# A four-layer streaming encoder on one core: the schedule form of each layer's head, zero-padded values for the sliding-window heads, and the norms' running sums on VectorE

## The chip, the core and the metric

The kernel runs on one core of a Trainium2 chip. The metric is device time in microseconds (us) of one execution; lower is better. Five engines work side by side, each on its own stream of instructions: PE (matrix multiplies, with its weight loads shown as PEld), DVE (VectorE), ACT (ScalarE), POOL (GpSimd) and SP (SyncE, which issues the transfers).

## The reference

One inference step with four layers over 320 tokens (256 of a prompt, 64 of a decoding stream), model width 1024. Each layer adds three things to the residual stream x:

```python
for i in range(DEPTH):                     # DEPTH = 4
    x = x + mixer_i(rms_norm(x, g_mix[i])) # i mod 3: 0 MLA, 1 stick-breaking (SBA), 2 sliding window (SWA)
    x = x + conv_ffn(rms_norm(x, g_ffn[i]), ...)
    x = x + sigmoid(rms_norm(x, g_ple[i]) @ w_gate[i]) * (p[i] @ w_proj[i])
y = rms_norm(x, g_final)
# rms_norm(x, g) = x * rsqrt(mean(x * x) + eps) * g
```

So the mixers in order are MLA, SBA, SWA, MLA. The last product of a layer, the gated one, is called PLE below. SWA has 16 query heads on 4 key heads of width 64, with 128 cached keys for the decoding stream. All is float32.

## The kernel before

**Layout.** x is kept transposed, as eight tiles x0 to x7 of 128 features by 320 tokens (NT). Each float32 matrix product is three matmuls on operands that were split into a high and a low part (`mm3`, L202 to L204: hi by hi, lo by hi, hi by lo), 24 matmuls for a full product of 1024 features into 128. Splits of anything are one ACT instruction for the high part (L160) and one subtraction for the low part (L161).

**Weights** come in 512 KB chunks (`fetch`, L168 to L176): a transfer into wraw, ACT makes whi, and DVE or POOL makes wlo (L176). POOL gets every second or third chunk while a mixer runs (`wpool`, set from WPOOL when the mixer begins) and none at other times.

**Norms.** The scale 1/rms isn't applied to the operand: products run on x times g and their results are multiplied by R, the scale spread over 128 partitions. For the norm of the next stage `norm_piece(m)` runs as soon as x[m] is final: ACT makes h{m}hi (L305), DVE h{m}lo (L306), ACT the square sq (L314), and the running sum acc is added on POOL for m = 1 to 6 (L320; m = 0 is a copy) and on DVE for m = 7. Then `norm_sums` lets PE add acc over partitions (`col_sums`, L272) and DVE find 1/rms on three columns ncol (`newton_rsqrt`, L252 to L258, eleven short instructions); `spread` puts it on the diagonal of two tiles (DVE, L282 and L283, also named sq), lets PE multiply them by ones (L287) and ACT copy R (L290).

**PLE** (`ple`, L406) goes over m: a 24-matmul product, times R (DVE L429), tanh (ACT L430), times the embedding's product (DVE L431), added to x[m] (DVE L433), then `norm_piece(m)` for the next mixer.

**Between layers.** `prep` of the next mixer (its caches' loads, splits and transposes) is called ahead of `ple`, so in program order ahead of that norm's sums. `swa_prep` loads and splits the cached keys and values; `mla_prep` transposes cached latents (`latent_turn`, L489). Their transposes use the two PSUM tiles of tag "tp", which `col_sums` and `spread` use too.

**Order.** A scheduler orders each engine's instructions by its own estimate; at a mixer's head PE has program order instead (`manual_schedule`): one full product on h0 to h7, `norm_sums`, more products, `norm_spread`. In SWA, `values(kt, i0)` multiplies the transposed softmax tiles by the values once for each of two heads u: each round fills two "tp" tiles and ends in three splits of 64 partitions into O.

## Time and profile before

| what | value |
|---|---|
| time, median of 3 runs | 1865.1 us (1860.9 to 1867.74) |
| profiled execution: its time, its span | 1871.49 us, 1869.7 us |
| busy in the span | PE 96%, DVE 72%, ACT 52%, POOL 30% |
| PE clock, mean over the span | 0.983 of full |

PE is busy nearly all the time, so the time is PE's work at the clock it was granted, plus its gaps. The stages by time: MLA 30 to 220 us, FFN to 476, PLE to 515; SBA to 680, FFN to 913, PLE to 953; SWA to 1090, FFN to 1325, PLE to 1364; MLA to 1590, FFN to 1822, PLE to 1856, final norm to 1869.7.

### The profile page before, as it was taken

Reading aid. Unit: us, or ns where it says so; the run is one execution under the profiler, and the core shown is the slowest. Engines: PE = TensorE matmul, PEld = TensorE weight load, DVE = VectorE, ACT = ScalarE, POOL = GpSimd, SP = SyncE. Lnnn points to the kernel's source line nnn. Section 1 sums busy time; section 2 is a strip of 40 time slices with the busy share of each in tenths; the row PEclk is TensorE's granted clock in tenths of the full one; section 3 lists DMA queues with packets and bytes.
Section 4 is the critical chain, followed back from the end, with each engine's and each line's share of the span. In section 5 each row is a group of like instructions: output and inputs, shape, how many; then the busy total and the mean of one; then the engine's idle time right before and its main releaser. Section 6 shows DMA issues by size and latency. Waiting matters only on the chain.

```text
span 1869.7 us, 32633 instructions
## 1 busy us (share of the span) xinstructions
PE 1798.8 (96%) x12352; PEld 1775.2 (95%) x12352; DVE 1347.4 (72%) x2637; ACT 974.6 (52%) x1849; POOL 565.6 (30%) x834
## 2 busy tenths in 40 slices
...
GB/s 207 107 112 124 126 138 162 151 150 149 168 128 140 121 133 152 151 148 150 126 157 76 46 143 158 148 154 150 144 124 100 122 129 122 157 147 153 153 147 63
DMA packets 78126, 254.15 MB, mean 136 GB/s; under 512 B 9488, under 2 KB 18192, under 8 KB 77968
## 3 DMA queue, kind: packets, MB, share of 16 engines
...
q14 instruction: 61, 0.50, 0.1%
...
## 4 chain that ended last, share of the span: by engine, by line
PE 41%; DVE 6%; ACT 2%; issue 1%; POOL 1%; DMA 0%; DVEq 0%; SPq 0%; ACTq 0%; POOLq 0%
PE ps L202 13%; PE ps L203 13%; PE ps L204 13%; ACT whi L174 1%; DVE rsh L596 1%; DVE wlo L176 1%; PE ps L272 0%; PE ps L1188 0%; DVE PTl L161 0%; POOL wlo L176 0%; DVE h6lo L306 0%; DVE m L1165 0%; DMA ckt<-ckvT 0%; DVE m L671 0%; ACT Pr L675 0%
## 5 line engine op out<-in xcount | busy, mean ns | idle before, releaser
L174 ACT ACTIVATE whi<-wraw 128x1024 fp32r<-128x1024 f32 x450 | 474.5, 1056 | 443.0 <-PE ps L203 230.4
L176 DVE TENSOR_TENSOR wlo<-wraw,whi 128x1024 fp32r<-128x1024 f32 x381 | 471.1, 1237 | 226.5 <-ACT whi L174 219.5
L176 POOL TENSOR_TENSOR wlo<-wraw,whi 128x1024 fp32r<-128x1024 f32 x69 | 166.9, 2418 | 311.0 <-ACT whi L174 292.8
L384 POOL TENSOR_TENSOR ge<-cv,R 128x256 f32<-128x256 f32 (+1 forms) x176 | 132.8, 774 | 92.8 <-ACT cv L381 92.3
L320 POOL TENSOR_TENSOR acc<-acc,sq 128x320 f32<-128x320 f32 x72 | 77.4, 1075 | 261.6 <-ACT sq L314 259.0
L347 DVE TENSOR_TENSOR x<-x,ps 128x320 f32<-128x320 f32 x128 | 61.1, 482 | 55.7 <-PE ps L204 55.4
L379 DVE SCALAR_TENSOR_TENSOR cv<-G,cols,cv 128x322 f32<-128x322 f32 x176 | 95.9, 552 | 2.4
L388 DVE TENSOR_TENSOR af<-ge,ps 128x320 f32<-128x320 f32 x88 | 42.7, 486 | 67.6 <-POOL ge L384 67.4
L202 PE MATMUL ps<-h0hi,whi 128*128 128x320 f32 x256 | 81.1, 317 | 6.5 <-ACT h0hi L305 6.2
L203 PE MATMUL ps<-h6lo,whi 128*128 128x320 f32 x256 | 79.4, 310 | 3.3 <-DVE h6lo L306 3.3
L202 PE MATMUL ps<-h7hi,whi 128*128 128x320 f32 x256 | 79.2, 311 | 3.3 <-ACT h7hi L305 3.3
L203 PE MATMUL ps<-h0lo,whi 128*128 128x320 f32 x256 | 79.9, 312 | 0.8 <-DVE h0lo L306 0.8
L202 PE MATMUL ps<-h4hi,whi 128*128 128x320 f32 x256 | 79.6, 313 | 1.1 <-ACT h4hi L160 1.1
L203 PE MATMUL ps<-h5lo,whi 128*128 128x320 f32 x256 | 79.4, 310 | 1.2 <-DVE h5lo L161 1.2
L203 PE MATMUL ps<-h7lo,whi 128*128 128x320 f32 x256 | 79.9, 312 | 0.5 <-DVE h7lo L306 0.5
L202 PE MATMUL ps<-h1hi,whi 128*128 128x320 f32 x256 | 79.9, 312 | 0.0
L203 PE MATMUL ps<-h4lo,whi 128*128 128x320 f32 x256 | 79.7, 311 | 0.2 <-DVE h4lo L306 0.2
L203 PE MATMUL ps<-h3lo,whi 128*128 128x320 f32 x256 | 79.9, 312 | 0.0
L203 PE MATMUL ps<-h2lo,whi 128*128 128x320 f32 x256 | 79.9, 312 | 0.0
L203 PE MATMUL ps<-h1lo,whi 128*128 128x320 f32 x256 | 79.8, 312 | 0.0
L204 PE MATMUL ps<-h1hi,wlo 128*128 128x320 f32 x256 | 79.8, 312 | 0.0
L204 PE MATMUL ps<-h0hi,wlo 128*128 128x320 f32 x256 | 79.8, 312 | 0.0
...
## 6 DMA issues: line engine op xcount, KB each, us to landing
...
```

What stands on the lines that cost most here:

```text
L174: nc.scalar.activation(out=hi, in_=raw, func=AF.Copy)
L176: e.tensor_tensor(out=lo, in0=raw, in1=hi.bitcast(F32), op=ALU.subtract)
L202: mm(out, w[0], x[0], start=first, stop=False, **kw)
L203: mm(out, w[0], x[1], start=False, stop=False, **kw)
L204: mm(out, w[1], x[0], start=False, stop=last, **kw)
L320: e.tensor_tensor(out=self.nacc[:, 0:NT], in0=self.nacc[:, 0:NT], in1=sq, op=ALU.add)
L347: self.nc.vector.tensor_tensor(out=self.x[m], in0=self.x[m], in1=p[:, 0:NT], op=ALU.add)
L379: nc.vector.scalar_tensor_tensor(out=cv, in0=gt[:, k:k + GW - 2], scalar=w[k], in1=cv, op0=ALU.mult, op1=ALU.add)
L384: nc.gpsimd.tensor_tensor(out=ge[:, c], in0=cv[:, c.start + o:c.stop + o], in1=R[:, c], op=ALU.mult)
L388: nc.vector.tensor_tensor(out=af, in0=ge, in1=pu[:, 0:NT], op=ALU.mult)
L596: nc.vector.tensor_tensor(out=lo[r, :].bitcast(F32R), in0=qf[r, :], in1=hi, op=ALU.subtract)
```

## The change

- **Running sums.** All additions of acc are on DVE. For m = 7 the square is made before the operand.
- **Diagonal.** The two diagonal tiles are made in `norm_sums`, right behind the Newton steps.
- **Heads.** SBA uses a new order (`head`): its first product A on h0 to h6, the second product B on h0 and h1, the sums, B on h2 to h6, and only then h7 for both. From PLE's last m up to this head all four engines keep program order. MLA keeps its order. SWA's hand-written order is gone: the scheduler orders it.
- **Weights.** `wpool` is set behind a mixer's head (`headed`), not when the mixer begins.
- **Preparation.** `prep` is called inside `ple`, behind that norm's spread. `swa_prep` does nothing any more: SWA loads its caches itself and splits a key head's old and new columns in one go (448 columns).
- **Values.** Each of a pair of SWA heads has its own value tile, zero in the other head's 64 columns, so both heads' products add up in one PSUM tile of 128 partitions: `values` has one round with three splits of 128 partitions, and the same number of matmuls.
- **Final norm.** POOL makes -x*g, DVE multiplies six of the eight outputs by the spread's PSUM result itself, and POOL two by R.

```diff
     def spread(self, r, pool, tag, bufs=2):
+        return self.spread_mm(self.diag(r), pool, tag, bufs)
+    def diag(self, r):
...
+        return dg
...
+    def spread_mm(self, dg, pool, tag, bufs=2, sign=-1.0):
+        nc = self.nc
         p = self.ps("tp")
         for k in range(2):
             i = nc.tensor.matmul(p[:, 0:NT], self.negones, dg[k], start=k == 0, stop=k == 1)
         self.pins.append(i)
         rb = self.tile(pool, [P, NT], tag, bufs=bufs)
-        nc.scalar.activation(out=rb, in_=p[:, 0:NT], func=AF.Copy, scale=-1.0)
+        self.negR = p[:, 0:NT]
+        nc.scalar.activation(out=rb, in_=p[:, 0:NT], func=AF.Copy, scale=sign)
...
+        if m == NK - 1:
+            self.norm_square(m)
+            self.norm_operand(m)
+        else:
+            self.norm_operand(m)
+            self.norm_square(m)
+    def norm_operand(self, m):
...
+            nc.gpsimd.tensor_scalar(out=hi, in0=x, scalar1=self.col(self.ng, m), scalar2=-1.0,
+                                    op0=ALU.mult, op1=ALU.mult)
...
+    def norm_square(self, m):
+        nc = self.nc
         sq = self.tile(self.nrm, [P, NT], "sq", bufs=2)
-        nc.scalar.activation(out=sq, in_=x, func=AF.Square)
+        nc.scalar.activation(out=sq, in_=self.x[m], func=AF.Square)
         if m == 0:
             self.nacc = self.tile(self.nrm, [P, NT + DEC], "acc", bufs=1)
             nc.gpsimd.tensor_copy(out=self.nacc[:, 0:NT], in_=sq)
         else:
-            e = nc.vector if m == NK - 1 or self.wpos == 0 else nc.gpsimd
+            e = nc.vector
             e.tensor_tensor(out=self.nacc[:, 0:NT], in0=self.nacc[:, 0:NT], in1=sq, op=ALU.add)
...
+        first = [(p, [self.take(name, np.arange(k * P, k * P + P), cols) for k in range(NK)]) for p, name, cols in (A,)]
+        mm = lambda n, k: self.mm3(first[n][0], first[n][1][k], h[k], k == 0, k == NK - 1)
+        for k in range(NK - 1):
+            mm(0, k)
+        p, name, cols = B
+        first.append((p, [self.take(name, np.arange(k * P, k * P + P), cols) for k in range(NK)]))
+        for k in range(NK - 1):
+            mm(1, k)
+            if k == 1:
+                self.norm_sums(keep_sum)
+        mm(0, NK - 1)
+        mm(1, NK - 1)
+        self.norm_spread()
+        self.proj(*C, h)
...
-            self.nr = self.newton_rsqrt(v)
+            self.nr = self.diag(self.newton_rsqrt(v))
     def norm_spread(self):
         with self.tc.high_priority(AHEAD):
-            self.R = self.spread(self.nr, self.nrm, "R")
+            self.R = self.spread_mm(self.nr, self.nrm, "R")
...
-        after()
+        prep = after()
...
+            if m == NK - 1 and nxt == 1:
+                self.region.enter_context(self.tc.manual_schedule(engines=ALL))
             pp = pps[m]
             pg = self.ps("mm")
             self.proj(pg[:, 0:NT], f"pg{i}", cols, h)
+            if m == NK - 1 and nxt == 1:
+                self.more_weights()
...
+        ps = [weighed(0, n) for n in range(3)]
+        self.head(*ps)
+        self.headed(1)
         with self.tc.manual_schedule(engines=PE):
-            pq, pk = project(0, 0), project(0, 1)
-            self.norm_sums()
-            pv = project(0, 2)
+            with self.tc.high_priority(AHEAD):
+                scaled(0, 0, ps[0][0])
+                scaled(0, 1, ps[1][0])
...
-            self.norm_spread()
+            scaled(0, 2, ps[2][0])
...
     def swa_prep(self, j, pool):
...
-        for kt in range(2):
-            kf, vf = T([P, W], f"kf{kt}"), T([P, W], f"vf{kt}")
-            nc.sync.dma_start(out=kf[:, NT:W], in_=t["wkT"][kt])
-            nc.sync.dma_start(out=vf[:, NT:W], in_=t["wvT"][kt])
-            KF.append(kf)
-            VF.append(vf)
-        self.load_rot(pool)
-        for kt in range(2):
-            kh = [pair([P, W], f"K{kt}{u}") for u in range(2)]
-            for u in range(2):
-                for x in kh[u]:
-                    nc.gpsimd.memset(x[64 * (1 - u):64 * (2 - u), :].bitcast(F32), 0.0)
-                s = slice(64 * u, 64 * u + 64)
-                self.split(kh[u][0][s, NT:], kh[u][1][s, NT:], KF[kt][s, NT:])
-            K.append(kh)
-            vh = pair([P, 4, P], f"V{kt}")
-            tp = self.ps("tp")
-            nc.tensor.transpose(tp[:, 0:P], VF[kt][:, NT:W], self.ident)
-            self.split(vh[0][:, 3], vh[1][:, 3], tp[:, 0:P])
-            V.append(vh)
-        return KF, VF, K, V
+        return None
...
-        early = {}
-        def product(m, tag="mm"):
-            p = self.ps(tag)
-            return p
-        with self.tc.manual_schedule(engines=PE):
-            for n, m in enumerate((8, 10, 0, 1, 2, 3)):
-                early[m] = product(m, "mm" if n < 3 else "sc")
-                if n == 1:
-                    self.norm_sums()
-                if n == 3:
-                    self.norm_spread()
+        self.headed(2)
+        h = self.norm_finish()
+        R = self.R
+        tags = ["sc"] * 3 + ["mm"] * 3
...
         def keys(kt):
-            kf, kh = KF[kt], K[kt]
+            kf = T([P, W], "kvf", bufs=2)
+            nc.sync.dma_start(out=kf[:, NT:W], in_=t["wkT"][kt])
             rope_bias(8 + kt, project(8 + kt), kf[:, 0:NT])
             nc.sync.dma_start(out=t["o_wk"][kt], in_=kf)
+            kh = [pair([P, W], f"K{kt}{u}") for u in range(2)]
             for u in range(2):
+                for x in kh[u]:
+                    nc.gpsimd.memset(x[64 * (1 - u):64 * (2 - u), :].bitcast(F32), 0.0)
                 s = slice(64 * u, 64 * u + 64)
-                self.split(kh[u][0][s, 0:NT], kh[u][1][s, 0:NT], kf[s, 0:NT])
+                self.split(kh[u][0][s, :], kh[u][1][s, :], kf[s, :])
+            K.append(kh)
         def vals(kt):
-            vf, vh = VF[kt], V[kt]
+            vf = T([P, W], "kvf", bufs=2)
+            nc.sync.dma_start(out=vf[:, NT:W], in_=t["wvT"][kt])
             f = project(10 + kt)
             nc.scalar.activation(out=vf[:, 0:NT], in_=f, func=AF.Identity, bias=self.col(f"bq{j}", 10 + kt))
             nc.sync.dma_start(out=t["o_wv"][kt], in_=vf)
-            pv = transposes([vf[:, c:c + P] for c in (0, P, S0 - 64)])[:, 0:3 * P]
-            self.split(vh[0][:, 0:3], vh[1][:, 0:3], pv.rearrange("p (a b) -> p a b", a=3))
+            vh = [pair([P, 4, P], f"V{kt}{u}") for u in range(2)]
+            for u in range(2):
+                for x in vh[u]:
+                    nc.gpsimd.memset(x[:, :, 64 * (1 - u):64 * (2 - u)].bitcast(F32), 0.0)
+            pv = four(transposes([vf[:, c:c + P] for c in (0, P, S0 - 64, NT)]))
+            for u in range(2):
+                c = slice(64 * u, 64 * u + 64)
+                self.split(vh[u][0][:, :, c], vh[u][1][:, :, c], pv[:, :, c])
+            V.append(vh)
...
-            vv = lambda b: [x[:, b] for x in V[kt]]
+            vv = lambda u, b: [x[:, b] for x in V[kt][u]]
             i2 = slice(i0, i0 + 2)
+            p, p2 = self.ps("tp"), self.ps("tp")
             for u in range(2):
-                s = slice(64 * u, 64 * u + 64)
-                p, p2 = self.ps("tp"), self.ps("tp")
-                self.mm3(p[:, 0:256], vv(0), [flat(x[:, 4 + u]) for x in PT], True, True)
+                self.mm3(p[:, 0:256], vv(u, 0), [flat(x[:, 4 + u]) for x in PT], u == 0, u == 1)
+            for u in range(2):
                 for b in range(2):
-                    self.mm3(p[:, 256:512], vv(b), [flat(x[:, 2 * u + b]) for x in PT], b == 0, b == 1)
+                    self.mm3(p[:, 256:512], vv(u, b), [flat(x[:, 2 * u + b]) for x in PT], u + b == 0, u + b == 2)
+            for u in range(2):
                 for b in range(2):
-                    self.mm3(p2[:, 0:P], vv(2 + b), [x[:, 2 * u + b] for x in PTs], b == 0, b == 1)
-                for c, src in ((slice(0, P), p[:, 0:256]), (slice(P, SEQ), p[:, 256:512]),
-                               (slice(S0, NT), p2[:, 0:P])):
-                    self.split(o[0][s, i2, c], o[1][s, i2, c], two(src)[s])
+                    self.mm3(p2[:, 0:P], vv(u, 2 + b), [x[:, 2 * u + b] for x in PTs], u + b == 0, u + b == 2)
+            for c, src in ((slice(0, P), p[:, 0:256]), (slice(P, SEQ), p[:, 256:512]), (slice(S0, NT), p2[:, 0:P])):
+                self.split(o[0][:, i2, c], o[1][:, i2, c], two(src))
...
+    def headed(self, kind):
+        self.region.close()
+        self.wpool = WPOOL[kind]
...
-            self.wpool = WPOOL[kind]
             (self.mla, self.sba, self.swa)[kind](j, pool, prep[1])
...
-            if last:
-                self.ple(i, ple, e, lambda: self.norm_start("g_final", None, None))
-            else:
-                prep = self.prep(self.layers[n + 1])
-                self.ple(i, ple, e, lambda: self.norm_start(f"g_mix{self.layers[n + 1]}"))
+            def after():
+                if last:
+                    return self.norm_start("g_final", None, None)
+                self.norm_start(f"g_mix{self.layers[n + 1]}")
+                return self.prep(self.layers[n + 1])
+            prep = self.ple(i, ple, e, after, None if last else MIXERS[self.layers[n + 1]][0])
             self.shut(cp)
...
-        self.norm_finish()
+        self.norm_sums()
+        R = self.spread_mm(self.nr, self.nrm, "R", sign=1.0)
         for m in range(NK):
             y = self.tile(self.hp, [P, NT], f"h{m}hi", bufs=1)
-            if m % 3 == 2:
-                nc.gpsimd.tensor_tensor(out=y, in0=self.fin[m], in1=self.R, op=ALU.mult)
+            if m % 4 == 2:
+                nc.gpsimd.tensor_tensor(out=y, in0=self.fin[m], in1=R, op=ALU.mult)
             else:
-                nc.vector.tensor_tensor(out=y, in0=self.fin[m], in1=self.R, op=ALU.mult)
+                nc.vector.tensor_tensor(out=y, in0=self.fin[m], in1=self.negR, op=ALU.mult)
```

How the order of instructions moves, at three places. In the rows the number at a name's end only tells buffers apart; line numbers of the changed kernel differ (L179 is L176, L205 to L207 are L202 to L204, L275 is L272, L325 is L306, L344 is L320, L486, L488 and L490 are L429, L431 and L433).

DVE at the end of the first layer's PLE, before: from h5's low part to the last sum.

```order
L306 SCALAR_TENSOR_TENSOR h5lo_6264<-x_13_97,gains_73,h5hi_6263 128x320
L431 SCALAR_TENSOR_TENSOR G_1278_6301<-G_1278_6301,ps_6170 128x320
L433 TENSOR_TENSOR x_14_99<-x_14_99,G_1278_6301 128x320
L429 TENSOR_TENSOR G_1286_6344<-ps_6313,R_5941 128x320
L306 SCALAR_TENSOR_TENSOR h6lo_6307<-x_14_99,gains_73,h6hi_6306 128x320
L431 SCALAR_TENSOR_TENSOR G_1286_6344<-G_1286_6344,ps_6220 128x320
L433 TENSOR_TENSOR x_15_101<-x_15_101,G_1286_6344 128x320
L306 SCALAR_TENSOR_TENSOR h7lo_6350<-x_15_101,gains_73,h7hi_6349 128x320
L320 TENSOR_TENSOR acc_6012<-acc_6012,sq_6353 128x320
```

The same place now, from the weight chunk ahead of h5's low part on (that chunk's wlo was POOL's before).

```order
L179 TENSOR_TENSOR wlo_6349<-wraw_6346,whi_6348 128x1024
L325 SCALAR_TENSOR_TENSOR h5lo_6264<-x_13_97,gains_73,h5hi_6263 128x320
L344 TENSOR_TENSOR acc_6012<-acc_6012,sq_6267 128x320
L488 SCALAR_TENSOR_TENSOR G_1278_6301<-G_1278_6301,ps_6170 128x320
L486 TENSOR_TENSOR G_1289_6352<-ps_6315,R_5906 128x320
L490 TENSOR_TENSOR x_14_99<-x_14_99,G_1278_6301 128x320
L488 SCALAR_TENSOR_TENSOR G_1289_6352<-G_1289_6352,ps_6220 128x320
L325 SCALAR_TENSOR_TENSOR h6lo_6307<-x_14_99,gains_73,h6hi_6306 128x320
L490 TENSOR_TENSOR x_15_101<-x_15_101,G_1289_6352 128x320
L344 TENSOR_TENSOR acc_6012<-acc_6012,sq_6310 128x320
L344 TENSOR_TENSOR acc_6012<-acc_6012,sq_6357 128x320
L325 SCALAR_TENSOR_TENSOR h7lo_6361<-x_15_101,gains_73,h7hi_6360 128x320
```

Three sums came to DVE here, the second half of m = 7's chain stands directly around h6's low part, and h7's low part is last.

PE at the head of SBA, before: the end of the first product, the sums, and the second product's begin.

```order
L202 MATMUL ps_6393<-h6hi_6306,whi_6316 128x320
L203 MATMUL ps_6393<-h6lo_6307,whi_6316 128x320
L204 MATMUL ps_6393<-h6hi_6306,wlo_6317 128x320
L202 MATMUL ps_6393<-h7hi_6349,whi_6316 128x320
L203 MATMUL ps_6393<-h7lo_6350,whi_6316 128x320
L204 MATMUL ps_6393<-h7hi_6349,wlo_6317 128x320
L272 MATMUL ps_6424<-ones_112,acc_6012 128x2 x3
L202 MATMUL ps_6450<-h0hi_6006,whi_6365 128x320
```

Now: the same first product stops at h6, and h7 comes 15 matmuls after the sums' three (at the "..." stand the rest of the second product's rows on h0 to h6).

```order
L207 MATMUL ps_6368<-h6hi_6306,wlo_6274 128x320
L205 MATMUL ps_6369<-h0hi_6006,whi_6318 128x320
...
L207 MATMUL ps_6369<-h1hi_6057,wlo_6319 128x320
L275 MATMUL ps_6404<-ones_112,acc_6012 128x2 x3
L205 MATMUL ps_6369<-h2hi_6113,whi_6318 128x320
...
L207 MATMUL ps_6369<-h6hi_6306,wlo_6319 128x320
L205 MATMUL ps_6368<-h7hi_6360,whi_6273 128x320
L206 MATMUL ps_6368<-h7lo_6361,whi_6273 128x320
```

The first row that needs h7 moved from 2 to 24 rows behind the one that needs h6's low part, the sums' row from 5 to 8 behind it.

PE at the head of SWA. Before, one product is finished alone, as in SBA (its rows for h6 and h7, the sums, and the next product).

```order
L203 MATMUL ps_11659<-h6lo_11573,whi_11582 128x320
L204 MATMUL ps_11659<-h6hi_11572,wlo_11583 128x320
L202 MATMUL ps_11659<-h7hi_11615,whi_11582 128x320
L203 MATMUL ps_11659<-h7lo_11616,whi_11582 128x320
L204 MATMUL ps_11659<-h7hi_11615,wlo_11583 128x320
L272 MATMUL ps_11690<-ones_112,acc_11278 128x2 x3
```

Now three products are interleaved: h6's low part is first used by the 40th matmul of the stage and h7 by the 50th.

```order
L205 MATMUL ps_11736<-h0hi_11229,whi_11629 128x320
L206 MATMUL ps_11626<-h6lo_11530,whi_11496 128x320
L207 MATMUL ps_11626<-h6hi_11529,wlo_11497 128x320
L206 MATMUL ps_11681<-h6lo_11530,whi_11539 128x320
L207 MATMUL ps_11681<-h6hi_11529,wlo_11540 128x320
L206 MATMUL ps_11736<-h0lo_11230,whi_11629 128x320
...
L205 MATMUL ps_11626<-h7hi_11575,whi_11496 128x320
L275 MATMUL ps_11585<-ones_112,acc_11235 128x2 x3
L206 MATMUL ps_11626<-h7lo_11576,whi_11496 128x320
```

The first use of h6's low part moved from the 20th matmul of the stage to the 40th, and that of h7 from the 22nd to the 50th.

## Rows read from the trace of the kernel before

**Rows 1.** The page: busy shares; one costly group with PE's idle time before it.

```profile
PE 1798.8 (96%) x12352; PEld 1775.2 (95%) x12352; DVE 1347.4 (72%) x2637; ACT 974.6 (52%) x1849; POOL 565.6 (30%) x834
...
L203 PE MATMUL ps<-h6lo,whi 128*128 128x320 f32 x256 | 79.4, 310 | 3.3 <-DVE h6lo L306 3.3
```

**Rows 2.** Windows by stage: length, busy times, granted clock, DMA share, GB/s.

```profile
220.00:476.00 256.00, 254.92 (x1739) 254.53 (x1738) 173.23 (x283) 110.83 (x161) 75.46 (x155) 1.00 0.45 151
476.00:515.00 39.00, 35.46 (x236) 34.22 (x235) 32.81 (x61) 21.43 (x38) 9.42 (x10) 0.99 0.48 156
...
913.00:953.00 40.00, 36.80 (x228) 36.28 (x228) 31.53 (x60) 19.48 (x34) 8.83 (x8) 0.91 0.40 128
...
975.00:1048.00 73.00, 62.59 (x378) 59.97 (x377) 56.19 (x182) 45.88 (x145) 31.82 (x34) 0.81 0.18 59
...
1325.00:1364.00 39.00, 36.40 (x234) 35.65 (x235) 32.12 (x61) 20.11 (x35) 8.75 (x8) 0.96 0.40 135
```

**Rows 3.** Timeline 508.0 to 516.6: start, duration, engine, instruction, idle before it.

```profile
508.33 0.31 PE L204 MATMUL ps<-ph7hi,wlo 128*128 128x320 f32 x1
...
509.72 2.39 POOL L176 TENSOR_TENSOR wlo<-wraw,whi 128x1024 fp32r<-128x1024 f32 x1 [1.61 <-ACT whi L174]
...
510.12 2.33 DVE L306 SCALAR_TENSOR_TENSOR h6lo<-x,gains,h6hi 128x320 fp32r<-128x320 f32 x1 [0.33 <-ACT h6hi L305]
...
512.51 0.41 PE L203 MATMUL ps<-h6lo,whi 128*128 128x320 f32 x1 [1.09 <-DVE h6lo L306]
...
514.18 0.41 PE L202 MATMUL ps<-h7hi,whi 128*128 128x320 f32 x1 [1.11 <-ACT h7hi L305]
```

**Rows 4.** Durations by line over the whole span: min/median/max in ns.

```profile
L306 DVE SCALAR_TENSOR_TENSOR h6lo<-x,gains,h6hi x8: 535/1198/2334, 12.2 to 1586.4; 128x320 fp32r<-128x320 f32 x8
...
L431 DVE SCALAR_TENSOR_TENSOR G<-G,ps x32: 473/482/489, 484.7 to 1853.9; 128x320 f32<-128x320 f32 x32
```

**Rows 5.** Durations of the running sum's additions, the same view for tile acc.

```profile
L320 POOL TENSOR_TENSOR acc<-acc,sq x72: 861/1034/1782, 230.8 to 1852.6; 128x320 f32<-128x320 f32 x72
L320 DVE TENSOR_TENSOR acc<-acc,sq x19: 474/481/493, 8.5 to 1855.6; 128x320 f32<-128x320 f32 x19
```

**Rows 6.** PE's timeline at the column sums of the second and third PLE.

```profile
914.00 1.44 PE L272 MATMUL ps<-ones,acc 128*128 128x2 f32 x6 [2.25 <-DVE V0l L161]
...
1325.23 0.83 PE L272 MATMUL ps<-ones,acc 128*128 128x2 f32 x6 [1.23 <-DVE Vl L161]
```

**Rows 7.** Windows over two stretches at the lower granted clock.

```profile
914.00:920.80 6.80, 6.80 (x27) 6.80 (x28) 3.29 (x18) 0.00 (x0) 0.00 (x0) 0.51 0.24 77
...
514.50:517.90 3.40, 3.23 (x13) 3.13 (x13) 1.84 (x3) 1.06 (x1) 0.00 (x0) 0.50 0.08 33
```

**Rows 8.** What PE waited for, 975 to 1048: total us, times, longest.

```profile
PE ps L202 <- ACT Pr L1173: 3.4, 3, 1.9
PE ps L1188 <- DVE su L1175: 2.3, 1, 2.3
...
PE ps L202 <- DVE O0l L161: 1.2, 2, 1.0
```

**Rows 9.** Groups by line, 975 to 1048: shapes, count, busy us, mean ns.

```profile
L161 DVE TENSOR_TENSOR O0l<-ps,O0h 64x256 fp32r<-64x256 f32 x8 | 3.3, 414 | 2.0 <-ACT O0h L160 1.8
```

**Rows 10.** Timeline 1861.9 to 1863.2: the first final outputs.

```profile
1861.97 0.44 ACT L290 ACTIVATE R<-ps 128x320 f32<-128x320 f32 x1 [6.45 <-PE ps L287]
1862.44 0.49 DVE L1341 TENSOR_TENSOR h0hi<-h0lo,R 128x320 f32<-128x320 f32 x1 [1.20 <-ACT R L290]
...
1862.85 1.15 DVE L1341 TENSOR_TENSOR h1hi<-h1lo,R 128x320 f32<-128x320 f32 x1
```

**Rows 11.** What PE waited for, 476 to 490.

```profile
PE ps L287 <- DVE sq L282: 0.9, 1, 0.9
```

**Rows 12.** The page: the groups that make wlo, count, busy us, mean ns.

```profile
L176 DVE TENSOR_TENSOR wlo<-wraw,whi 128x1024 fp32r<-128x1024 f32 x381 | 471.1, 1237 | 226.5 <-ACT whi L174 219.5
L176 POOL TENSOR_TENSOR wlo<-wraw,whi 128x1024 fp32r<-128x1024 f32 x69 | 166.9, 2418 | 311.0 <-ACT whi L174 292.8
```

45 lines of the change are left out of this document (25 added, 20 removed).

## The prediction

> **What bounds the kernel now.** I read the page first: PE is busy 96% of the span, DVE 72% [rows 1]. So the time is PE's work plus what PE loses, and the change leaves PE's matmuls as they are. The most to be won is PE's idle time, 1869.7 - 1798.8 = 71 us, and what the lower clock costs, (1 - 0.983) x 1869.7 = 32 us.
>
> The windows by stage come next, to see where that loss lies. An FFN loses 1 us of 256 at full clock, and there a matmul takes 254.92 / 1739 = 0.147 us of PE [rows 2]. The loss sits around the changes of layer and in SWA: 40 - 36.8 = 3.2 us idle and (1 - 0.91) x 40 = 3.6 us of clock around the change to SWA; 10.4 idle and 0.19 x 73 = 13.9 of clock in SWA's core; 2.6 and 1.6 around the change to the last MLA; 3.5 idle around the change to SBA [rows 2].
>
> The timeline at 510 us shows why PE stops when a mixer begins. POOL's wlo runs 509.72 to 512.11; DVE's h6 low part, issued beside it, takes 2.33 us and ends when wlo ends; PE, which goes through h0 to h7 in one product, waits 1.09 us for it. x7 is then late, so h7's high part is late, and PE waits 1.11 us more [rows 3]. Alone the same DVE instruction takes 0.535 us [rows 4]. The same pair stands at the two later changes of layer: the page gives 3.3 us of waiting for h6's low part in all [rows 1], three times 1.1. PE's clock then fell to 0.50 for 3.4 us after the first of the three places [rows 7]; after the other two it did not.
>
> What POOL delays is a DVE instruction whose tensors all lie in SBUF. Those that read one tensor from PSUM never grew, 473 to 489 ns in 32 cases, POOL busy or not [rows 4]. The Trainium skill, page SBUF — State Buffer, section Who interferes with whom, says the same as a rule: a DVE instruction with two SBUF inputs and a GpSimd instruction that reads SBUF block one another, and the first keeps the way for its whole length. The trace agrees.
>
> The third kind of loss is in the PLE. The column sums wait for a "tp" tile that the next mixer's preparation holds: 2.25 us before SWA, 1.23 us before the last MLA [rows 6]. After the first PE ran 6.8 us at 0.51 of its clock, which costs half of it, 3.4 us [rows 7]; after the second the 1.6 us above.
>
> **The change, part by part.**
>
> *Sums on DVE.* 72 additions leave POOL (1.034 us each) and come to DVE at 0.481 us [rows 5]: 72 x 0.481 = 35 us more on DVE. What hides them is PE: no sum is awaited before the column sums, and DVE is idle 28% of the span. The tightest place is a PLE, DVE 32.81 of 39 us [rows 2]: six additions there are 2.9 us, within the 6.2 us left. Without cover they would cost 2.9 us per PLE. What the additions on POOL had made longer on DVE comes back to it; I don't count that. I take 0.
>
> *Change to SBA.* The POOL wlo ahead of the head goes to DVE, 1.24 us [rows 12], but it stands ahead of h5's low part and not beside h6's. PE reached its wait at 512.51 - 1.09 = 511.42. The last gate product ends at 508.6 [rows 3]; from there DVE's new order has its step times R, x6, the step with the embedding, and h6's low part, 0.4 to 0.55 us each, with tanh and h6's high part on ACT between them, some 0.5 us each: about 511.2, so the first wait goes by a margin of 0.2 us. h7 is wanted 15 matmuls after the sums (2.2 us) and is long there. Gain: 1.1 + 1.1 of waits and 1.7 of clock (half of 3.4 [rows 7]) = 3.9 us. Bounds: all of it, or only 1.1 where DVE is one wlo later. The wait of the spread in the same PLE, 0.9 us [rows 11], stays, since a wlo and splits of the caches still stand ahead of the Newton steps. The new head puts transposes of the first values close behind the products that they need; that wait the trace doesn't show, 0 to one POOL wlo (2.4 us [rows 12]); I take 0.9 as in [rows 11], the nearest wait of PE for DVE.
>
> *Change to SWA.* With no preparation the 2.25 us and the 3.4 us of clock go. The wlo on POOL stays and h6's low part will again take 2.33 us, but it is wanted 20 matmuls later (20 x 0.147 = 2.9 us) and h7 28 later (4.1 us): both waits of 1.1 us are covered. Gain 2.25 + 3.4 + 2.2 = 7.9 us; at least 5.7, if the interleaving doesn't cover.
>
> *SWA's core.* 24 low splits of 64 partitions become 12 of 128; at 0.414 us, less for the narrow third of them, DVE loses some 4.5 us of work, and ACT about as much for the high parts [rows 9]. DVE is busy 56.2 of 73 us there [rows 2] and PE waits for it and for ACT behind it: 3.4 for the exponentials, 2.3 for a softmax sum, 1.2 for the splits of the first of two rounds [rows 8], which now don't exist. Against it: the cached columns are split here now (128 more columns, four times, some 0.15 us each), two splits of values per key head in place of one, 16 fills with zeros on POOL. Bounds: two thirds of the 24 us lost there (-16), or the low clock for another 16 us (+8). I take what DVE saves, with the half of a gap that it causes at the low clock: -5.
>
> *Change to the last MLA.* The column sums no longer stand behind the preparation: 1.2 + 1.6 = 2.8 us (bounds 1.2 and 2.8). The two waits at the mixer's begin stay: its product order is as before, and the wlo that POOL no longer makes there stands on DVE between the steps of x6.
>
> *Final norm.* DVE no longer waits for ACT's R (0.44 us) and reads PSUM, so the outputs that took 1.15 us beside POOL take 0.49 [rows 10]: 0.44 + 2 x 0.66 = 1.8, less what PE and the last transfer take of it: -1.5 (bounds -0.5 and -1.8).
>
> *Sum:* -3.9 + 0.9 - 7.9 - 5 - 2.8 - 1.5 = -20.2 us. Against the profiled execution, 1871.5 - 20.2 = 1851.3; that execution lies 6.4 us above the median of the runs, so I expect **1845 us**.
>
> **The rivals.**
>
> *B: SWA gives nothing, and SBA's first wait stays.* For it: the margin of 0.2 us there, and that SWA's waits are for a chain of softmax steps which the change doesn't shorten [rows 8]. 1845 + 5 + 2.8, and up to 4 more: 1853 to 1860.
>
> *C: SWA's clock stays up.* If the waits in its core become short, most of the 13.9 us comes back: -16 in place of -5, 1834. For it: PE falls to the low clock only behind waits; against it: only 1.2 us of them certainly go [rows 8].
>
> *D: DVE's sums become the bound at the mixers' ends (slower).* The added instructions have all tensors in SBUF, and POOL still makes wlo there. If all 24 of them in the four mixers ran beside one, they would take 2.33 in place of 0.48 us, 44 us in all. DVE's 28% idle over eight output steps of 24 to 48 matmuls (28 to 56 us a mixer) is 8 to 16 us a mixer; with half of the 44 us at the wrong place and the clock low for 6.8 us behind each, the loss is 22 + 4 x 3.4 = 35 us: 1880. It decides from about four of six additions blocked in a mixer. Against it: POOL's wlo takes 167 us [rows 12] of 718 us of mixers, not quite a quarter, so some six of 24 meet one. By the skill's rule above the same follows: every such addition is open to blocking; here it would be worth some 6 us of DVE under cover.
>
> *E: nothing.* PE's stalls move to the next late thing (the gain in a PLE is waited off at the mixer's begin): 1861 to 1867. Against it: the FFNs behind run at full clock with no loss [rows 2], so time won before them isn't given back in them.
>
> **How the numbers follow.** Mine 0.55 (its own range 1837 to 1853, from the bounds of SWA, -12 to +2, which are the widest); B 0.18; C 0.12; D 0.07; E 0.08. Half a per cent, about what can be told from no change, is 9.3 us: 1855.8 and 1874.4. Faster: mine, C and half of B, 0.76. Same: the other half of B and E, 0.17. Slower: D, 0.07. The range 1831 to 1862 holds mine, B, most of C and a little of E, about 0.82.
>
> **What would show it.** In the profile after: no wait for h6's low part or h7's high part at the begin of SBA and SWA, but both still at the last MLA; column sums of the second and third PLE without a wait and their stretches at full clock; POOL with only m = 0's copy of acc; DVE's busy time some 20 to 25 us higher; in SWA's core, a granted clock above 0.81 and half as many splits into O. I am wrong if SWA's core is as long as before, if new waits for DVE stand at SBA's begin, or if additions of acc take over 1 us in most cases.

## The result and the profile after

The changed kernel takes 1849.88 us (median of 4 runs, 1847.58 to 1851.6) where the kernel before took 1863.0 beside it: ratio 0.9913, 95% interval 0.9893 to 0.9933. The two medians alone give 0.9930, which lies inside that interval. It is faster by 0.7 to 0.9%, between the 1845 that was predicted and the upper end of the range. In the 49 runs of the kernel before that were made beside the later kernels the median is 1866.9 us, so the gain is 13 to 17 us, by which of the two one takes. The two profiled executions differ by more, 1869.7 - 1848.5 = 21.2 us of span, since that of before, 1871.5 us, was longer than any of these 49. Left out of all comparisons are two runs, one of E10 (its only profiled one, so that E10 has no stages below) and one of the kernel before, which ran at a mean granted clock of 0.653 and took some 2480 us.

The page of the changed kernel, busy shares as in [rows 1]:

```profile
PE 1786.0 (97%) x12352; PEld 1762.6 (95%) x12352; DVE 1353.3 (73%) x2697; ACT 969.5 (52%) x1833; POOL 483.1 (26%) x766
```

POOL's busy time fell by 82 us, DVE's rose by 6, not by the 35 of the additions alone.

Windows of the changed kernel over the stages of [rows 2] (length, PE, PEld, DVE, ACT, POOL busy, granted clock, DMA share, GB/s):

```profile
475.00:511.00 36.00, 35.56 (x240) 34.74 (x239) 30.94 (x66) 19.89 (x36) 0.70 (x3) 1.00 0.46 151
511.00:675.00 164.00, 160.06 (x1084) 153.64 (x1083) 137.85 (x259) 123.20 (x270) 39.07 (x28) 1.00 0.37 123
...
908.00:946.00 38.00, 38.00 (x263) 38.00 (x262) 31.43 (x65) 19.90 (x34) 3.83 (x4) 1.00 0.46 153
946.00:1069.00 123.00, 112.40 (x794) 110.73 (x794) 101.25 (x275) 78.47 (x211) 50.04 (x64) 0.94 0.28 93
...
1302.00:1341.00 39.00, 37.56 (x253) 36.42 (x251) 33.24 (x70) 22.11 (x39) 0.65 (x1) 1.00 0.46 150
```

The second PLE has no loss left (38.00 of 38.00 us at full clock, where [rows 2] had 3.2 idle and 0.91). New is the second line: in SBA, where PE had hardly a gap behind the head before, it now has 3.9 us of them.

PE's timeline of the changed kernel at SBA's head (h6's low part, the column sums), and at the column sums of the second and third PLE ([rows 3, 6]):

```profile
509.76 0.41 PE L206 MATMUL ps<-h6lo,whi 128*128 128x320 f32 x1
...
511.34 0.80 PE L275 MATMUL ps<-ones,acc 128*128 128x2 f32 x6
...
910.99 0.73 PE L275 MATMUL ps<-ones,acc 128*128 128x2 f32 x6
...
1304.49 0.72 PE L275 MATMUL ps<-ones,acc 128*128 128x2 f32 x6
```

None of these rows has a wait of note in front of it (none shows an idle time in brackets): the waits of 1.09, 2.25 and 1.23 us are gone. DVE's timeline there shows why the first is:

```profile
509.15 0.55 DVE L325 SCALAR_TENSOR_TENSOR h6lo<-x,gains,h6hi 128x320 fp32r<-128x320 f32 x1
509.62 0.48 DVE L490 TENSOR_TENSOR x<-x,G 128x320 f32<-128x320 f32 x1
```

h6's low part takes 0.55 us, no longer 2.33, and PE reads it as it ends.

Durations by line in the changed kernel, answering to [rows 4, 5]: h6's low part (eight norms) and the additions of acc.

```profile
L325 DVE SCALAR_TENSOR_TENSOR h6lo<-x,gains,h6hi x8: 534/544/1993, 12.2 to 1566.9; 128x320 fp32r<-128x320 f32 x8
...
L344 DVE TENSOR_TENSOR acc<-acc,sq x91: 474/484/2699, 8.5 to 1835.9; 128x320 f32<-128x320 f32 x91
```

The median of h6's low part fell from 1198 to 544 ns. Of the 91 additions three ran beside a wlo of POOL and took 2.7 us.

What PE waited for in SWA, 941 to 1069 us of the changed kernel ([rows 8]):

```profile
PE ps L1227 <- DVE PTl L164: 6.8, 2, 5.7
PE ps L205 <- ACT Pr L1212: 2.4, 1, 2.4
PE ps L207 <- POOL Ql L164: 0.9, 1, 0.9
```

The waits for O0's splits are gone. Those for transposed softmax tiles, of which before had these,

```profile
PE ps L202 <- DVE PTl L161: 1.7, 1, 1.7
...
PE ps L1188 <- DVE PTl L161: 0.7, 2, 0.4
```

have grown into one of 5.7 us. The final outputs ([rows 10]), timeline of the changed kernel:

```profile
1841.59 0.44 ACT L301 ACTIVATE R<-ps 128x320 f32<-128x320 f32 x1 [5.76 <-PE ps L297]
...
1842.06 0.49 DVE L1386 TENSOR_TENSOR h0hi<-h0lo,ps 128x320 f32<-128x320 f32 x1 [1.19 <-ACT R L301]
1842.46 0.48 DVE L1386 TENSOR_TENSOR h1hi<-h1lo,ps 128x320 f32<-128x320 f32 x1
```

No output is stretched to 1.15 us any more, but DVE still starts only when ACT's copy ends, though it reads PSUM.

**Stages.** The comparisons below go by PE's own records: the start of the last matmul of each FFN's output (on a*hi), of each gate product (on ph7hi) and of each attention output (on O*h). In the changed kernel these starts are 469.54, 506.67, 672.13, 905.12, 941.28, 1065.64, 1298.63 and 1336.14 us. Differences of them are the lengths of stages; "end" runs from the last gate matmul to the end of the span. The stages that are left out (the two MLA stages with their FFNs, the FFNs behind SBA and SWA, the last PLE) make up the rest. In us, one profiled execution each:

| kernel | PLE0 and SBA | PLE1 | SWA | PLE2 | end | median of runs | ratio to before |
|---|---|---|---|---|---|---|---|
| before | 201.2 | 42.0 | 136.8 | 39.6 | 17.1 | 1866.9 | 1 |
| changed | 202.6 | 36.2 | 124.4 | 37.5 | 15.7 | 1849.9 | 0.9913 |
| E1 SBA's old head | 201.1 | 36.2 | 124.6 | 37.5 | 15.7 | 1848.3 | 0.9915 |
| E2 sums on POOL | 202.0 | 36.2 | 122.7 | 38.0 | 16.4 | 1850.9 | 0.9925 |
| E3 values unpadded | 202.8 | 36.2 | 130.0 | 37.4 | 16.3 | 1856.2 | 0.9953 |
| E4 preparation in front | 202.0 | 36.2 | 124.0 | 39.8 | 16.3 | 1852.5 | 0.9932 |
| E5 SWA ordered by hand | 202.8 | 36.2 | 124.8 | 37.4 | 16.3 | 1852.0 | 0.9928 |
| E6 SWA's caches in PLE | 203.2 | 36.5 | 123.6 | 37.3 | 15.7 | 1849.3 | 0.9915 |
| E7 old head, late POOL share | 200.9 | 36.2 | 123.9 | 37.4 | 16.3 | 1848.0 | 0.9904 |
| E8 sums twice | 203.0 | 36.2 | 124.4 | 37.7 | 16.1 | 1865.1 | 0.9996 |
| E9 split head | 199.6 | 36.2 | 124.1 | 37.6 | 15.7 | 1846.3 | 0.9888 |
| E11 before, preparation behind | 201.0 | 36.4 | 131.0 | 37.3 | 17.1 | 1858.8 | 0.9954 |
| E12 before, two parts | 199.6 | 36.7 | 125.2 | 37.6 | 17.1 | 1853.3 | 0.9945 |

The ratios' intervals reach 0.0013 to 0.0025 to either side, and the ratios were measured beside runs of the kernel before, so they are the safer comparison between kernels. Where an edit doesn't touch it, PLE1 repeats much better: it is 36.16 us in nine of them. SWA does not, since PE's clock falls there for 6.8 to 27.3 us, which differs from execution to execution.

### The profile page after: what moved, and what is told of

Same layout as the page of the kernel before. It is cut to its first block, busy times and chain, and to the rows that moved or that the text cites. A ratio compares the mean times of both kernels' runs of the same rounds, so it can differ in the third digit from the quotient of the medians.

```text
span 1848.5 us, 32578 instructions
## 1 busy us (share of the span) xinstructions
PE 1786.0 (97%) x12352; PEld 1762.6 (95%) x12352; DVE 1353.3 (73%) x2697; ACT 969.5 (52%) x1833; POOL 483.1 (26%) x766
## 4 chain that ended last, share of the span: by engine, by line
PE 81%; DVE 10%; ACT 5%; issue 2%; DMA 1%; POOL 1%; DVEq 0%; SPq 0%; ACTq 0%; POOLq 0%
PE ps L205 26%; PE ps L206 26%; PE ps L207 26%; ACT whi L177 2%; DVE wlo L179 1%; DVE rsh L654 1%; DMA wraw<-w 1%; PE ps L753 1%; PE ps L275 0%; ACT Pr L733 0%; PE ps L700 0%; DVE qnl L164 0%; PE ps L701 0%; DVE KR L541 0%; DVE PTl L164 0%
## 5 line engine op out<-in xcount | busy, mean ns | idle before, releaser
L179 DVE TENSOR_TENSOR wlo<-wraw,whi 128x1024 fp32r<-128x1024 f32 x385 | 475.0, 1235 | 220.3 <-ACT whi L177 213.0
L179 POOL TENSOR_TENSOR wlo<-wraw,whi 128x1024 fp32r<-128x1024 f32 x65 | 157.5, 2423 | 380.5 <-ACT whi L177 340.0
L436 POOL TENSOR_TENSOR ge<-cv,R 128x256 f32<-128x256 f32 (+1 forms) x176 | 141.4, 823 | 86.4 <-ACT cv L433 86.1
L431 DVE SCALAR_TENSOR_TENSOR cv<-G,cols,cv 128x322 f32<-128x322 f32 x176 | 97.2, 560 | 2.3
L205 PE MATMUL ps<-h0hi,whi 128*128 128x320 f32 x256 | 81.1, 317 | 6.8 <-ACT h0hi L324 6.2
L205 PE MATMUL ps<-h4hi,whi 128*128 128x320 f32 x256 | 79.8, 313 | 1.1 <-ACT h4hi L163 1.1
L205 PE MATMUL ps<-h6hi,whi 128*128 128x320 f32 x256 | 79.3, 311 | 1.0 <-ACT h6hi L324 1.0
L205 PE MATMUL ps<-h2hi,whi 128*128 128x320 f32 x256 | 79.7, 311 | 0.0
L207 PE MATMUL ps<-h1hi,wlo 128*128 128x320 f32 x256 | 79.7, 311 | 0.0
L205 PE MATMUL ps<-h1hi,whi 128*128 128x320 f32 x256 | 79.6, 311 | 0.0
L207 PE MATMUL ps<-h0hi,wlo 128*128 128x320 f32 x256 | 79.6, 311 | 0.0
```

What stands on the lines that cost most here:

```text
L179: e.tensor_tensor(out=lo, in0=raw, in1=hi.bitcast(F32), op=ALU.subtract)
L205: mm(out, w[0], x[0], start=first, stop=False, **kw)
L207: mm(out, w[1], x[0], start=False, stop=last, **kw)
L431: nc.vector.scalar_tensor_tensor(out=cv, in0=gt[:, k:k + GW - 2], scalar=w[k], in1=cv, op0=ALU.mult, op1=ALU.add)
L436: nc.gpsimd.tensor_tensor(out=ge[:, c], in0=cv[:, c.start + o:c.stop + o], in1=R[:, c], op=ALU.mult)
```

## The experiments

The theory is the prediction's sum. Its main rival after the result came from the stages: SBA had not gained 3.0 us but lost 1.4 with its PLE, while SWA had gained 12.4 in place of 7.2.

**E1. SBA's old head.**

```diff
-        ps = [weighed(0, n) for n in range(3)]
-        self.head(*ps)
         self.headed(1)
         with self.tc.manual_schedule(engines=PE):
+            pq, pk = project(0, 0), project(0, 1)
+            self.norm_sums()
+            pv = project(0, 2)
...
```

In PLE the lines that put SBA's head into program order on four engines go too, with a call that fetches weights there (`more_weights`).

> The changed kernel with SBA as before: its head in the old order (first product on h0 to h7 in one go, sums behind two products), no stretch in program order on four engines, POOL's share of the weights set when SBA begins. By the prediction's step the new head is worth 3.9 - 0.9 = 3.0 us, so the time goes from 1849.9 up to about 1853, and the two waits of 1.1 us for h6's low part and h7's high part come back. The rival, from the trace after: SBA from PLE's last gate matmul to its last output matmul took 163.4 us before and 165.5 after, so the new head gave back more in SBA's core than it won at its begin; then the time falls to about 1848 and the waits of PE for su, A2's low part and sp0's low part between 569 and 630 us (2.8 us) go.

Measured: 201.1 us for PLE0 and SBA, 1.5 less than the changed kernel; 1848.3 us. What PE waited for from 470 us to SBA's end:

```profile
PE ps L206 <- DVE h6lo L325: 1.4, 1, 1.4
PE ps L205 <- ACT h7hi L324: 0.9, 1, 0.9
PE ps L205 <- ACT O7h L163: 0.8, 1, 0.8
```

and the same stretch of the changed kernel (475 to 675):

```profile
PE ps L205 <- DVE A2l L164: 1.3, 2, 0.7
PE ps L205 <- DVE su L1024: 0.9, 2, 0.5
PE ps L205 <- ACT O7h L163: 0.8, 1, 0.8
PE ps L1036 <- DVE sp0l L164: 0.6, 2, 0.4
```

The rival holds in its result: the new head makes SBA slower. In the seven profiled executions that have it, PLE0 and SBA take 202.0 to 203.2 us, in the five with the old one 199.6 to 201.2. The waits listed don't give the size, for the new head removes 2.2 us of waits (1.4 + 0.9) and 1.7 us of low clock, and the core puts only 2.8 us (1.3 + 0.9 + 0.6) in their place. Windows over 130 us of the core, from 20 us behind the last gate matmul, first of E1, then of the changed kernel, show the rest:

```profile
525.50:655.50 130.00, 130.00 (x900) 127.18 (x899) 112.38 (x212) 108.23 (x243) 32.64 (x19) 1.00 0.39 131
```

```profile
526.70:656.70 130.00, 127.02 (x862) 121.55 (x861) 111.01 (x202) 102.68 (x233) 30.11 (x18) 1.00 0.38 126
```

PE has 38 matmuls fewer in the same time, at 130 / 900 = 0.144 us some 5.5 us, more than its 3.0 us of idle time: a matmul's record is 0.31 us long where the next one follows after 0.15 us, so the first part of each wait counts as busy. The 5.5 us stand against the 3.9 that the head won.

The two cores also differ in more than what stands ahead of them. By PE's records from the last gate matmul to SBA's last output matmul, E1 and E7 have the same 1089 matmuls in the same order, E1 and the kernel before have an unbroken run of 1074 in common, and E1 and the changed kernel none longer than 80. With the new head the scheduler made another order of the whole core. No run has the new head with the old core's order, so whether the core takes back time or is only ordered worse is open.

**E2. Sums on POOL.**

```diff
-            e = nc.vector
+            e = nc.vector if m == NK - 1 or self.wpos == 0 else nc.gpsimd
```

> The changed kernel with the additions of acc for m = 1 to 6 on POOL again, nothing else. By the prediction the 35 us that they are on DVE lie under PE's work: no change, 1848 to 1852, with DVE's busy time some 25 us lower. Rival 1: DVE's load is felt in the PLEs and in SBA, then 2 to 4 us faster (1846 to 1848). Rival 2: the additions on POOL block the operands' low parts at the mixers' begins, then the waits for h6's low part come back and it is 2 to 5 us slower (1852 to 1855).

Measured: 1850.9 us, the stages within 1.7 us of the changed kernel's, some up and some down. DVE's busy time is 1339.7 in place of 1353.3 us: 72 additions cost DVE 13.6 us net. They give back about 21 of their 34.6 us in less blocking: the low parts of h and ph, which take 77.9 us here, take 56.5 in the changed kernel. The low parts of h6:

```profile
L325 DVE SCALAR_TENSOR_TENSOR h6lo<-x,gains,h6hi x8: 539/703/2344, 12.3 to 1564.0; 128x320 fp32r<-128x320 f32 x8
```

The longest, 2.34 us, stands at SWA's head, where the changed kernel has 1.99 us and PE waits in neither. Only at the last MLA a wait for h6's low part is back, 1.3 us; with that for h7's high part it makes 2.1 us, and the changed kernel waits 1.9 us at the same place (h6's high part 1.0, h7's low part 0.5, h6's low part 0.4). So the sums on DVE are worth nothing that can be measured, either way. Neither rival's time came.

**E3. Values unpadded.**

```diff
-            vh = [pair([P, 4, P], f"V{kt}{u}") for u in range(2)]
...
+            vh = pair([P, 4, P], f"V{kt}")
...
-            vv = lambda u, b: [x[:, b] for x in V[kt][u]]
+            vv = lambda b: [x[:, b] for x in V[kt]]
...
             for u in range(2):
...
+                s = slice(64 * u, 64 * u + 64)
+                p, p2 = self.ps("tp"), self.ps("tp")
...
```

> The changed kernel with one value tile per key head as before and two rounds of values, each with three splits of 64 partitions; the rest of SWA as changed. By the prediction's step the padding is worth the 5 us of SWA's core: SWA goes from 124.4 to about 129.4 us and the time to 1855. The rival: what shortened SWA is the order of its instructions, not the number of splits; then SWA stays within 1 us of 124.4 and the time within 1849 to 1851. A third: padding gave all that the prediction left out too, SWA 134 us, 1860.

Measured: SWA 130.0 us, 5.7 more; 1856.2 us. PE's waits in SWA (941 to 1075) that the changed kernel doesn't have:

```profile
PE ps L1222 <- DVE O0l L164: 2.2, 2, 1.5
...
PE ps L205 <- DVE O0l L164: 1.0, 1, 1.0
PE ps L205 <- ACT O1h L163: 0.7, 1, 0.7
```

DVE is busy 106.5 us in SWA in place of 102.1, so it saved 4.4 us where the prediction said 4.5, and PE spends the same 13.6 us at half clock in both, so the clock has no part in the 5.7. The step of 5 us is right, and so is its mechanism, DVE's saved work and PE waiting between two rounds for the splits of the first.

**E4. Preparation in front of the norm.**

```diff
+            nprep = None if last else self.prep(self.layers[n + 1])
             def after():
...
-                return self.prep(self.layers[n + 1])
+                return nprep
```

> The changed kernel with the next mixer's preparation called ahead of PLE's norm again (SBA's and the last MLA's; SWA has none). By the prediction the third PLE gets its wait of 1.2 us and 1.6 us at the low clock back: from 37.5 to 40.3 us, the time to 1852.7. From the stages of the two traces it is 2.1 us, 1852. The rival: that wait is absorbed at the last MLA's begin, where PE waits for h6 and h7 anyway; then the time stays at 1850.

Measured: the third PLE 39.8 us, 2.3 more; 1852.5 us. The wait is back, with 3.4 us at half clock behind it:

```profile
1307.15 0.83 PE L275 MATMUL ps<-ones,acc 128*128 128x2 f32 x6 [1.37 <-DVE Vl L164]
```

**E5. SWA's products ordered by hand.**

```diff
-        h = self.norm_finish()
+        h = self.nh
...
+        with self.tc.manual_schedule(engines=PE):
+            for n, m in enumerate((8, 10, 0, 1, 2, 3)):
+                early[m] = product(m, "mm" if n < 3 else "sc")
+                if n == 1:
+                    self.norm_sums()
+                if n == 3:
+                    self.norm_spread()
         R = self.R
...
```

> The changed kernel with SWA's products ordered by hand as before (a full product, a second one, the sums, two more, the spread, two more), values padded and no preparation, as changed. By the prediction the interleaving is worth the two waits of 1.1 us at SWA's begin: SWA from 124.4 to 126.6 us (and up to 3.4 us more if the clock falls behind them). The rival: the scheduler's order is worth all that the padding is not, 12.4 - 5.7 = 6.8 us; then SWA takes 131 us. If the order is worth nothing, SWA stays at 124.

Measured: SWA 124.8 us, 0.4 more than the changed kernel. The two waits are there (941 to 1070):

```profile
PE ps L206 <- DVE h6lo L325: 1.1, 1, 1.1
PE ps L205 <- ACT h7hi L324: 0.9, 1, 0.9
```

They are paid, and what makes up for them is the clock. PE spent 6.8 us of this SWA at half clock, the changed kernel 13.6. A window over the stage, whose counterpart of the changed kernel stands further down:

```profile
940.20:1064.90 124.70, 113.06 (x804) 110.20 (x803) 99.75 (x275) 78.21 (x210) 55.09 (x66) 0.97 0.29 98
```

Half clock costs half its time, so this execution lost 3.4 us less to it. At the same clock the hand order would take 0.4 + 3.4 = 3.8 us more (an estimate from these two executions); whether the clock stayed up by the order or by chance isn't known. The medians, 1852.0 and 1849.9 us, point the same way. The 2.2 us that the prediction gives to the interleaved head are not refuted.

**E6. SWA's caches prepared in the PLE, behind the spread.**

```diff
     def swa_prep(self, j, pool):
-        return None
...
+        for kt in range(2):
...
+            nc.tensor.transpose(tp[:, 0:P], VF[kt][:, NT:W], self.ident)
...
+                self.split(kh[u][0][c, NT:], kh[u][1][c, NT:], KF[kt][c, NT:])
...
```

> The changed kernel with SWA's cached keys and values loaded, transposed and split in the second PLE again, but called behind that norm's spread, and with the padded value tiles. If the 5.9 us that the second PLE won are due to the place of the preparation, PLE stays at 36.2 us and SWA may gain up to 1 us from work done earlier: 1848.5 to 1850. If they are due to its absence (its work on DVE, ACT and the tp tiles), PLE goes up by 2 us or more, with the wait for a tp tile now at another place: 1852 or more.

Measured: PLE1 36.5 us, SWA 123.6, 1849.3 us. The place of the preparation made the loss, not its work.

**E7. Old head, POOL's share set behind it.** As E1, with `self.headed(1)` moved behind the head.

> The changed kernel with SBA's head in the old order and without the stretch in program order, but POOL's share of the weights set only behind the head: POOL makes no wlo beside h6's low part. By the mechanism of the prediction both waits (1.4 and 0.9 us) and the 1.7 us at the low clock go. If SBA's core can use time won at its begin, SBA falls from 163.5 to about 159.6 us and the time to 1845. If the core gives it back (a chain on DVE and ACT bounds its rounds), SBA stays between 163 and 165.5 us and waits of PE for su, A2's and sp0's low parts appear.

Measured: 200.9 us, as E1. The wait for h6's low part only fell to 0.8 us and that for h7's high part rose to 1.3; PE's clock still fell behind them. The waits did not go, so this run doesn't tell the two cases apart.

**E8. Sums twice.** It adds work whose result nobody reads.

```diff
             e.tensor_tensor(out=self.nacc[:, 0:NT], in0=self.nacc[:, 0:NT], in1=sq, op=ALU.add)
+            if self.wpos:
+                two = self.tile(self.nrm, [P, NT], "sq2", bufs=1)
+                e.tensor_tensor(out=two, in0=self.x[m], in1=sq, op=ALU.add)
```

> The changed kernel with a second DVE instruction of the same size behind each addition of acc (x plus the square into a scratch tile, which nothing reads), outside the first norm: 84 instructions, 40 us more on DVE. If the additions lie under PE's work with room to spare, the time stays within 2 us of the changed kernel (PLE 36.2 to 37.5 us each). If DVE is at the edge in the PLEs, each of the four PLEs grows by 1 to 3 us and the mixers' begins wait for h6 and h7: 1855 to 1862.

Measured: 1865.1 us, 15 more, and not where either case expected it: the PLEs are unchanged, and the second and third FFN grow from 233.0 to 237.1 and 237.3 us (the two MLA stages with their FFNs grow by 2.3 and 4.3). There PE waits for DVE's evictions of the first products (timeline):

```profile
699.48 0.61 PE L205 MATMUL ps<-h0hi,whi 128*128 128x320 f32 x1 [2.52 <-DVE G L425]
```

In the changed kernel the last addition of this norm ends 6.1 us behind SBA's last output matmul and R is begun at 19.4; here they come at 9.6 and 22.8 us. So the cover is thin at one place, the begin of an FFN, where seven sums, the Newton steps and the new weights' low parts follow one another on DVE. One set of additions fits there, two don't.

**E9. Split head: h7 last for two products, the rest of SBA's head as before, POOL's share set behind it as in E7.**

```diff
+            ps = [weighed(0, n) for n in range(2)]
...
+            for ks in (range(NK - 1), (NK - 1,)):
+                for (q, _, _), y in zip(ps, wt):
+                    for k in ks:
+                        self.mm3(q, y[k], h[k], k == 0, k == NK - 1)
+            self.norm_sums()
+            pv = project(0, 2)
...
```

> As the run with SBA's old head and POOL's late share, but the first two products both stop at h6 and h7 comes for both of them behind that; sums, further products and SBA's core in the old order. PE's wait for h7's high part (1.3 us) must go, and with it probably the 1.7 us at the low clock; that for h6's low part (0.8 us) may stay. If SBA's core can use the time won at its begin, SBA falls from 163.3 to 160.4 to 162 us and the time to 1845 to 1846. If the core gives back whatever comes earlier, SBA stays at 163 or more with new waits of PE for DVE between 560 and 640 us.

Measured: 199.6 us for PLE0 and SBA, 3.0 less than the changed kernel and 1.3 less than E7. The wait for h7 and the low clock are gone, 3.0 us, and more than half of it comes back as new waits (470 to 674):

```profile
PE ps L205 <- DVE su L1019: 1.4, 3, 0.9
PE ps L206 <- DVE h6lo L325: 0.8, 1, 0.8
PE ps L205 <- ACT O7h L163: 0.5, 1, 0.5
```

E9's core, too, has an order of its own: its longest run of matmuls in common with E7 is 144. Its 1846.3 us is the lowest median of all, 0.9888 (0.9872 to 0.9904). That beats the kernel before; against the changed kernel the intervals overlap.

**E10. The kernel before with padded values alone** (the edit of E3 the other way round).

> The kernel before with the padded values alone (one round of values, three splits of 128 partitions; the caches still prepared in the second PLE). Undone in the changed kernel the padding cost SWA 5.7 us. If the parts of SWA add up, SWA falls here from 136.8 to 131.1 us and the time to 1858 to 1860. If the padding takes most of SWA's time at the low clock away by itself (27 us at half clock before, 14 in the changed kernel with or without it), SWA falls to 126 to 128 us, and the time to 1854 to 1856.

Measured: 1855.9 us, ratio 0.9937 (0.9918 to 0.9957). The time is that of the second case: alone, the padding is worth 8 to 15 us by the interval, more than the 5.7 us that it costs to undo it. That the rest is clock in SWA is not shown, since there are no stages of it.

**E11. The kernel before with the preparation behind the norm.**

```diff
-        after()
+        prep = after()
...
+                def after():
+                    self.norm_start(f"g_mix{self.layers[n + 1]}")
+                    return self.prep(self.layers[n + 1])
```

> The kernel before with one change: the next mixer's preparation is called behind PLE's norm and not ahead of it. The waits of the column sums for a tp tile (2.25 and 1.23 us) and the low clock behind them must go: second PLE from 42.0 to 36.2 us, third from 39.6 to 37.5, in all 8 us, the time to about 1857. If what is won there is waited off at the mixers' begins, the following SWA and MLA stages grow by as much, and the time stays above 1862. If SWA also loses its long stretch at the low clock, SWA falls below 134 us.

Measured: PLE1 36.4 and PLE2 37.3 us, 7.9 us less together; 1858.8 us, 8.1 less than before. In this execution SWA lost less to the clock too, 13.7 us at half clock in place of 27.3, and took 131.0 us.

**E12. The kernel before with both parts, E10 and E11.**

> The kernel before with two of the parts and nothing else: the padded values, and the next mixer's preparation (SWA's too) behind PLE's norm. If these two carry the whole gain, the time is that of the changed kernel, 0.991 of the kernel before (1848 to 1852), with the second PLE at 36.4, SWA at 124 to 126, the third PLE at 37.4, SBA at 163.4 and the end at 17.1 us; sums on DVE, new heads and the rest then sum to nothing. If the other parts carry a share of their own in SWA (the interleaved head, 2.2 us and the clock behind it) or at the end, the time is 1854 or more.

Measured: 0.9945 (0.9925 to 0.9965), 1853.3 us; PLE1 36.7, SWA 125.2, PLE2 37.6. The profiled spans, 1869.7 to 1850.5, would give the two parts 19 of the 21 us, but this execution is among the fastest of E12's eight and that of before the slowest of its kernel. By the medians they make 13.6 of 17.0 us, by the ratios 0.55 of 0.87%, and the intervals of E10, E12 and the changed kernel overlap. The time lies between the two cases of the expectation and decides neither: 3 to 6 us are left for the other parts by these two measures, and the intervals allow nothing at all. What the stages show of them is FFNs of 233.3 in place of 233.0 us and an end of 17.1 in place of 15.7 us.

## Why the prediction was right, and where not

**Right, by its own steps.** The column sums' waits: 42.0 to 36.2 us in the second PLE (5.9, said 5.65) and 2.1 in the third (said 2.8); E4, E6 and E11 show that it is the place of the preparation. The padded values: 5.7 us (said 5), by the work and the waits that were named, E3. The sums on DVE: nothing (said 0), E2; DVE's busy time rose by 6 and not by 20 to 25 us, because more blocking went than I had counted. SBA's head: the margin of 0.2 us held, PE came to h6's low part 0.06 us behind its end.

**Right in number, by luck: the end.** It is 1.4 us shorter, 1.5 were said. The outputs that POOL no longer stretches are done 1.3 us sooner behind R, as said, but the span ends 0.6 us later behind the last of them. The 0.44 us of DVE's wait for ACT's R were not won: DVE still waits, and why is open. The other 0.7 us come ahead of R, where the prediction had nothing: R begins 8.7 us behind the last gate matmul in place of 9.4, and in E2, E3, E4, E5 and E7 it begins at 9.3 to 9.4 again.

**Wrong: the change to SBA.** The step was "gain 1.1 + 1.1 of waits and 1.7 of clock", less 0.9. The three things went as said. What failed is that the sum has no term for SBA's core: it took the core for unchanged, without a reason, though a scheduler orders it anew, and the PLE with SBA took 1.4 us more, not 3.0 less. Rival E had the stalls move on, but only as far as to a gain of nothing. The core ran without a stall of PE, but for 0.8 us at its end that all have, in the kernel before, in E1, E7, E11 and E12; in the changed kernel it loses some 5.5 us, E1. E12 shows the price too, for in its execution the clock happened to stay up: with both waits at the head, 2.2 us, it takes 199.6 us, 3.0 less than the changed kernel without them. DVE's groups by line, 550 to 640 us, first of the changed kernel (a low part of the keys, the scan of su, a low part of A1):

```profile
L164 DVE TENSOR_TENSOR KTl<-kvf,KTh 128x320 fp32r<-128x320 f32 x5 | 6.4, 1271 | 1.7 <-ACT KTh L163 1.7
L1022 DVE TENSOR_TENSOR_SCAN su<-e,su,zeros 128x256 f32<-128x256 f32 x6 | 6.2, 1036 | 0.1
...
L164 DVE TENSOR_TENSOR A1l<-e,A1h 128x256 fp32r<-128x256 f32 x5 | 2.1, 420 | 0.0
```

and of E12:

```profile
L161 DVE TENSOR_TENSOR A1l<-e,A1h 128x256 fp32r<-128x256 f32 x7 | 5.1, 735 | 0.0
...
L962 DVE TENSOR_TENSOR_SCAN su<-e,su,zeros 128x256 f32<-128x256 f32 x6 | 4.4, 738 | 0.0
L161 DVE TENSOR_TENSOR KTl<-kvf,KTh 128x320 fp32r<-128x320 f32 x5 | 4.4, 874 | 0.2
```

The keys and the scan take 0.3 to 0.4 us longer each behind the new head, A1's low part 0.3 us less. POOL makes about as many wlo in SBA (15 in the changed kernel, 16 in E1 and E12), but beside other instructions, and PE waits for su among those that are longer. That this is the cause is not shown: the order of the core changed with the head (E1), and no run moved order or POOL alone.

**Not for the reason given: the size of SWA.** It won 12.4 us where 2.2 + 5 were said, and the clock makes the difference. Windows over the whole of SWA, of before, the changed kernel and E12:

```profile
947.00:1083.90 136.90, 123.12 (x801) 118.84 (x800) 103.15 (x282) 81.92 (x220) 52.47 (x48) 0.90 0.25 84
```

```profile
941.30:1065.70 124.40, 113.80 (x804) 112.14 (x804) 102.15 (x275) 78.28 (x210) 53.31 (x66) 0.95 0.30 98
```

```profile
941.00:1066.00 125.00, 113.81 (x799) 110.99 (x798) 99.02 (x270) 77.68 (x212) 52.99 (x49) 0.96 0.27 91
```

PE was at half clock for 27.3 us of SWA before and for 13.6 us after, which costs half of it, 13.7 and 6.8 us. So 6.8 us of the 12.4 are clock, and without it SWA is 5.6 us shorter, less than the 7.2 said. Likewise without its clock SWA is 5.7 us longer in E3, 3.8 in E5 and 2.5 in E12, which has the old head: by these single executions the padding and the interleaved head each give at least what was said. Together only 5.6 us came, so something is lost again in SWA; where is open. Rival C had the clock, to the full, as less likely; half of it came. By the runs the padding alone is worth 11.0 us (1866.9 - 1855.9), the preparation's place alone 8.1, and both together 13.6, less than their sum; that each alone already takes a part of the low clock away fits E11's SWA, and is not shown for the padding.

**Left out: the last MLA.** The prediction has no term for it behind the sums, and the waits at its begin stay, as said, 1.9 us. With its FFN it took 1.0 us more than before (460.6 in place of 459.6), with 3.4 us more at half clock.

**The total** was right to 5 us by luck, because the losses in SBA (4.4 us from what was said) and in the last MLA stood against SWA's clock: -20.2 said, -21.2 between the profiled spans, -13 to -17 by the runs. By the mean granted clocks, 0.984 in the middle run of before and 0.990 in the changed kernel's, some 11 of these us are clock, where the prediction counted 6.7 by name and an unnamed part of SWA's 5. Rival B's sum, 1845 + 5 + 2.8 and up to 4 more, ends at 1857 and not at 1860; nothing hangs on it. Rival D's mechanism exists (three additions of 2.7 us) at a small part of its price; E8 shows that its place is the FFN's begin.
